# Bias tables, reciprocals and pieces of v in fewer, larger transfers, with v in DRAM by columns of the grid

## The chip, the cores and the metric

The kernel runs on one core of a Trainium2 chip. The time is the device time of one execution in microseconds (us). The engines of the core are PE (TensorE, the matmuls; PEld is its weight load), DVE (VectorE), ACT (ScalarE), POOL (GpSimd) and SP (SyncE), which does no arithmetic here and issues the transfers (DMAs) between DRAM and the on-chip buffers. The transfers run on 16 DMA engines that all queues share.

## The reference, cut to what matters

One layer with two parallel branches over 512 tokens (8 rows by 64 columns of a grid) and 1024 channels. The input is normalised, scaled and shifted to h; h goes through eight projections of 1024 columns each, and the branches meet in a gated sum, an output projection and a final norm.

```
h = rms_norm(x, g_pre) * (1 + scl) + shift
xa, za, q, k, v, zb, ga, gb = split(h @ w_in)
y_a = recurrence(conv(xa)) * silu(za) @ w_pa
y_b = neighbourhood_attention(q, k, v, rpb) * silu(zb) @ w_pb
merged = sigmoid(ga) * y_a + sigmoid(gb) * y_b
out = rms_norm(x + gate * (merged @ w_o), g_final)
```

In the attention (16 heads of 64 channels) each token looks at all 8 rows and at a window of 16 columns near its own. Scores get a bias from `rpb`, by the difference of rows and of columns; the softmax is taken over the 128 keys of the window.

## The kernel before, in words

Every matmul product is formed from a high and a low part of both operands: three passes, hi*hi, hi*lo, lo*hi. A projection by one 128-column tile of a weight (`proj`, line 689) loads 512 KB (`wraw`), casts it on ACT (`whi`), takes the difference on DVE or POOL (`wlo`), and then issues 24 matmuls of 512 columns into one bank called `acc`.

The program comes from a planner (`Plan`, line 99): each piece of work is an `op` with an engine, an estimated cost, a rank and its buffers, and the planner simulates the engines and gives each engine a fixed order. Loads have ranks that say how far ahead of their use they go, and `after`, which holds them until a given projection has begun (`gate_of`). SBUF is cut into `NS` slots of 512 columns and `NW` slots of 1024. All loads and stores but two are issued by SP, in its fixed order. Transfers use eight completion semaphores in turn (the planner keeps as many lanes, line 264), so that a transfer is issued only when the one eight places ahead of it has landed.

The order of the work:

- h is formed, and v = h @ w_v is accumulated in eight banks (`hx`), 128 tokens by 512 channels each.
- `vout` (line 666) copies each bank as high and low parts, side by side, into `va` (128 tokens by 1024 numbers) and stores it to DRAM, in `vscr0` (heads 0 to 7) or `vscr1` (heads 8 to 15). This is eight stores of 512 KB.
- For each group g of two pairs of heads there are six projections (q, k, z of each pair, lines 939 to 947), then the scores of both pairs, and the softmax and the product with v (`attend`), mixed by the planner with the projections of the next group. `bias` (line 722) loads the bias table of a pair (`braw`), from which POOL makes three tiles `nb` by subtraction from a mask.
- `load_v` (line 750) reads v back from `vscr` in the form that the product wants, with the 128 partitions holding 16 columns of the grid by 8 rows: eight tiles `vt` for each group, for four blocks of queries. Two of the tiles are half zero, by a memset on POOL.
- The reciprocals of the softmax sums are put into DRAM (`rscr`, line 894) and read back as `rcx`, each row to 64 partitions (lines 895 to 897).
- After that come the recurrent branch, mixed with the product by `w_pb`, the gates, the product by `w_pa`, and the output.

The first six projections are named here by their place: q0, k0, z0 of the first pair, q1, k1, z1 of the second. The weights of q0, k0, z0 and q1 are loaded before the eight stores of v, and those of k1 and z1 behind them in SP's order.

Of the kernel before, what the change touches and what calls it, by code (L numbers as in the profile page):

```python
# [13 lines left out]
P = 128  # L14
S = 512
# [11 lines left out]
BIG = 1e30  # L27


NS, NW = 36, 32  # L30
WARM = 60

SLACK = 3
QP, QE, BD = 1, 1, 0
LIMITS = {"hx": 8, "acc": 3, "sp": 8, "pt": 2, "pv": 2, "mi": 2, "hd": 3, "gt": 8}


# [295 lines left out]
def layer(ctx, tc, x, x_t, par, w_m, w_g, bc_gate, w_v, w_in, w_blk, rpb, amask, w_pa, w_pb, w_o, g_final, out):  # L333
# [8 lines left out]
    def op(eng, cost, fn, rank, name="", **kw):  # L342
        return pl.op(eng, cost, fn, HEAD.get(name, rank), name=name, **kw)
# [7 lines left out]
    def T(name, dt=F32):  # L351
        return pl.tile("s", lambda i: sb.tile([P, S], dt, tag=f"s{i}", name=nm(name)))

    def W(name, dt=F32):
        return pl.tile("w", lambda i: sb.tile([P, D], dt, tag=f"w{i}", name=nm(name)))
# [15 lines left out]
    def load(t, dst, src, rank, size, after=(), spare=0, r=(), late=0.0, name="load"):  # L371

        return op("SP", 0.45, lambda e: nc.sync.dma_start(dst(), src() if callable(src) else src), rank,  # L373
                  r=r, w=[t], after=after, spare=spare, size=size, late=late or SLACK * (rank > 7.9), name=name)
# [8 lines left out]
    def mm(o, a, b, first, last):  # L383
        nc.tensor.matmul(o, a, b, start=first, stop=last)  # L384
# [6 lines left out]
    def whole(t):  # L391
        return lambda: t.ap
# [268 lines left out]
    main.append(ops[4])  # L661


    vscr = [pl.fixed(dp.tile([2, S, 512], F32, name=f"vscr{n}")) for n in range(2)]

    def vout(u, rank):
        n, t = u
        a = W("va", F32R)

        def view(off, step):  # L670
            part = list(a.ap.ap)[0]
            return bass.AP(a.ap.tensor, a.ap.offset + off, [part, [256, 4], [step, 2], [1, 64]])
        src = lambda: vps[u].ap.rearrange("p (a b c) -> p a b c", a=4, b=2)
        op("ACT", act(512), lambda e: nc.scalar.copy(view(0, 192), src()), rank, r=[vps[u]], w=[a], name="voh")
        op("DVE", dve(512), lambda e: nc.vector.tensor_tensor(view(64, 64), src(), view(0, 192).bitcast(F32), op=ALU.subtract),
           rank, r=[vps[u]], rw=[a], name="vol")
        dst = vscr[n].ap[:, t * P:(t + 1) * P, :].rearrange("g p c -> p g c")
        op("SP", 0.6, lambda e: nc.sync.dma_start(dst, a.ap.bitcast(F32).rearrange("p (g c) -> p g c", g=2)), rank - 3,
           r=[a], w=[vscr[n]], size=524288, name="vout")

    for u in VU:
# [2 lines left out]
    def gate_of(n, back):  # L684
        return [main[max(0, n - back)]] if n - back >= 0 else []
# [36 lines left out]

    def bias(pr, rank, after):
        raw = T("braw")
        rv = lambda: raw.ap.rearrange("p (h f) -> p h f", h=2)
        base = RPB_L - 1 - (PAD + 2 * pr * RPB_N + RPB_C * (ROWS - 1) + 7 + 255)
        for h in range(2):
            src = bass.AP(rpb.tensor, rpb.offset + base - h * RPB_N, [[RPB_C, ROWS], [1, 16], [1, 256]])
            load(raw, lambda h=h: rv()[:, h, :], src, rank - 4, 131072, after=after, spare=4, name="bias")
        res = []  # L730
        for v0, w, m0 in ((0, 32, 0), (8, 24, 32), (0, 24, 56)):
            nb = T("nb")
            res.append(nb)
            for h in range(2):
                def f(e, h=h, nb=nb, v0=v0, w=w, m0=m0):
                    part = list(raw.ap.ap)[0]
                    mv = msk.ap[:, m0:m0 + w].unsqueeze(1).to_broadcast([P, ROWS, w])
                    view = bass.AP(raw.ap.tensor, raw.ap.offset + h * 256 + 255 - v0, [part, [-RPB_C, ROWS], [-1, w]])
                    o = nb.ap.rearrange("p (h f) -> p h f", h=2)[:, h, :ROWS * w].rearrange("p (r c) -> p r c", c=w)
                    nc.gpsimd.tensor_tensor(o, mv, view, op=ALU.subtract)  # L740
                op("POOL", pool_(ROWS * w), f, rank - 1, r=[raw, msk], w=[nb], after=after, spare=2, name="nb")
        return res
# [4 lines left out]

    PIECES = {0: ((0, 0), (16, 0)), 1: ((8, 0), (24, 0)), 2: ((24, 0), (40, 0)), 3: ((40, 64), (48, 0))}

    def load_v(g, after):  # L750
        for b in (0, 3, 1, 2):
            for j, (c0, r0) in enumerate(PIECES[b]):

                a = vt[g, b, j] = T("vt", F32R)
                n = 64 if (b, j) in ((0, 1), (3, 0)) else P
                src = vscr[g // 2].ap[g % 2].rearrange("(r c) n -> c r n", r=ROWS)[c0:c0 + n // 8]
                load(a, lambda a=a, r0=r0, n=n: a.ap[r0:r0 + n, :].bitcast(F32), src, 8 + 6 * g - 1.5 + 0.1 * (b > 0), n * 2048,
                     r=[vscr[g // 2]], after=after, spare=3, name="vt")
                if n == 64:
                    op("POOL", 0.7, lambda e, a=a, r0=r0: nc.gpsimd.memset(a.ap[64 - r0:P - r0, :].bitcast(F32), 0.0), 8 + 6 * g - 1.5,  # L760
                       w=[a], after=after, spare=3, name="vz")

    ybh, ybl = {}, {}
    rcs = [const(f"rc{i}", [P, 32]) for i in range(2)]
# [39 lines left out]
    def attend(pr, sps, z, nbt, pos, pos0):  # L804
# [3 lines left out]
        def half(bs):  # L808
# [10 lines left out]
            for members in groups:  # L819
# [12 lines left out]
                for i, (b, h) in enumerate(members):  # L832
                    def f(e_, i=i, b=b, h=h, pv2=pv2):
                        c = 2 * bs.index(b) + h
                        nc.scalar.activation(pv2(i), pv2(i), AF.Exp, bias=mn.ap[:, c:c + 1], scale=-1.0,  # L835
                                             accum_out=sm.ap[:, 2 * b + h:2 * b + h + 1])
                    op("ACT", act(nk, 1, True), f, rk - 0.25, r=[mn, pt_], w=[pt_, sm], name="exp")
                ptp, nt = B("pt"), nk // 64

# [14 lines left out]
                def f(e_, members=members, ppv=ppv):  # L854
                    for i, (b, h) in enumerate(members):
                        e = bs.index(b)
                        for j in range(2):
                            mm(pv[h].ap[:, e * 256:(e + 1) * 256], vt[pr // 2, b, j].ap[:, off + h * P:off + (h + 1) * P],
                               ppv()[:, (i if edge else 2 * i) + j].rearrange("p s q -> p (s q)"), j == 0, j == 1)
                op("PE", 0.49, f, rk - 0.4, r=[pp] + [vt[pr // 2, b, j] for b in dict(members) for j in range(2)],  # L860
                   w=[pv[h] for h in dict((h, b) for b, h in members)], name="pv")

            vp = T("vp")
# [28 lines left out]
        scr = pl.fixed(dp.tile([32, P], F32, name=f"rscr{pr}"))  # L892
        op("DVE", 0.5, recip, pos - 0.3, r=[sm], w=[rc, rct], name="rc")
        op("SP", 0.5, lambda e: nc.sync.dma_start(turned(scr.ap), rct.ap[:, :32]), pos - 3, r=[rct], w=[scr], size=16384, late=SLACK, name="rcs")
        for h in range(2):
            src = bass.AP(scr.ap.tensor, scr.ap.offset + h * P, [[0, 64], [2 * P, 4], [1, P]])
            load(rcx, lambda h=h: rcx.ap[H[h], :].rearrange("p (b q) -> p b q", b=4), src, pos - 3, 131072, r=[scr], name="rcl", late=1.0)
        op("DVE", dve(512), lambda e: nc.vector.tensor_tensor(rbc(sz.ap), rbc(sz.ap), nat(rcx.ap), op=ALU.mult),
           pos - 0.3, r=[rcx], rw=[sz], lock=True, name="szr")
        op("DVE", dve(512), lambda e: nc.vector.tensor_tensor(rbc(sz.ap), nat(yt.ap), rbc(sz.ap), op=ALU.mult), pos + 0.5, r=[yt],  # L900
# [36 lines left out]
    for g in range(4):  # L937
        sets, zs, nbs = [], [], []
        for pr in (2 * g, 2 * g + 1):
            n0 = len(main)  # L940
            nbs.append(bias(pr, n0 + BD * (1 - pr % 2), gate_of(n0, 2) if pr else [main[6]]))
            if pr % 2 == 0:
                load_v(pr // 2, gate_of(n0, 2) if pr else [])
            q = proj(w_in[16 + pr], hhl, hll, LO_A if pr else "DVE")
            k = proj(w_in[24 + pr], hhl, hll, LO_A)
            zs.append(proj(w_in[32 + pr], hhl, hll, LO_A))
            sets.append(split(q, k))
        pos = k[0] + 0.6 + QP
        for i, sps in enumerate(scores(sets, pos, ends[-1:] if QE else [])):
            attend(2 * g + i, sps, zs[i], nbs[i], pos + 3 * i, pos)  # L950
# [378 lines left out]
```

## Time and profile before

| | us |
|---|---|
| median of 3 runs (lowest, highest) | 561.11 (560.77, 564.41) |
| the profiled execution's own time | 561.85 |
| its span in the profile | 560.1 |
| PE busy in the span | 550.8 |
| DVE, ACT, POOL busy | 392.7, 322.1, 99.0 |
| transfers of SP's queue | 82.76 MB, 45.2% of the 16 engines' span |

The times in the profile start at the span's start. A row of the chain of waits or of the timeline gives the start, the duration, the engine, the line, what was written from what, and how many instructions stand behind it. A row of a view by windows gives the busy time of each engine in that window with its instructions, the granted share of the TensorE clock, the mean busy share of the 16 DMA engines, and the GB/s that they moved.

### The profile page before, as it was taken

Reading aid. Unit: us, or ns where it says so; the run is one execution under the profiler, and the core shown is the slowest. Engines: PE = TensorE matmul, PEld = TensorE weight load, DVE = VectorE, ACT = ScalarE, POOL = GpSimd, SP = SyncE. Lnnn points to the kernel's source line nnn. Section 1 sums busy time; section 2 is a strip of 40 time slices with the busy share of each in tenths; the row PEclk is TensorE's granted clock in tenths of the full one; section 3 lists DMA queues with packets and bytes.
Section 4 is the critical chain, followed back from the end, with each engine's and each line's share of the span. In section 5 each row is a group of like instructions: output and inputs, shape, how many; then the busy total and the mean of one; then the engine's idle time right before and its main releaser. Section 6 shows DMA issues by size and latency. Waiting matters only on the chain.

```text
span 560.1 us, 7705 instructions
## 1 busy us (share of the span) xinstructions
PE 550.8 (98%) x2773; PEld 458.0 (82%) x2773; DVE 392.7 (70%) x712; ACT 322.1 (58%) x560; POOL 99.0 (18%) x97
## 2 busy tenths in 40 slices
PE   8999999999999999999999999999999999999995
PEld 8888888788888888887887888888788888888885
DVE  5998723684884886897569648866967897469523
ACT  6542523862763763777965984995698243223243
POOL 1102539453553540000000000000000000000220
PEclk9999999999999999999999999999999999999998
DMA  8993899439249244034333134032319452380002
GB/s 302 409 407 109 308 272 286 128 109 235 66 120 248 59 135 149 2 97 151 112 113 95 39 112 142 28 114 75 114 59 361 144 188 75 130 321 1 0 39 113
DMA packets 36509, 83.58 MB, mean 149 GB/s; under 512 B 4607, under 2 KB 11895, under 8 KB 36471
## 3 DMA queue, kind: packets, MB, share of 16 engines
q1 hardware_dynamic: 36192, 82.76, 45.2%
q8 instruction: 22, 0.36, 0.3%
q10 hardware_dynamic: 279, 0.32, 0.2%
q14 instruction: 16, 0.13, 0.1%
HBM read 76.65 MB, written 6.42 MB: 148 GB/s over the span
## 4 chain that ended last, share of the span: by engine, by line
PE 96%; DMA 2%; DVE 0%; SPq 0%; ACT 0%; POOL 0%; issue 0%; POOLq 0%
PE acc L384 78%; PE hx L384 8%; PE pv L384 3%; PE pt L842 2%; PE gt L384 2%; PE sp L384 2%; DMA wv<-in_w_v_dram 1%; DMA xT<-in_x_t_dram 1%; SPq L373 0%; POOL vl L381 0%; PE mi L384 0%; DVE yo L1216 0%; ACT vh L378 0%; DVE pp L850 0%; ACT pp L848 0%
## 5 line engine op out<-in xcount | busy, mean ns | idle before, releaser
L384 PE MATMUL acc<-hhl,whi 128*128 128x512 f32 x784 | 244.7, 393 | 0.0
L384 PEld LDWEIGHTS acc<-hhl,whi 128*128 128x128 f32 x784 | 143.7, 188 | 27.6 <-issue 0.4
L384 PE MATMUL acc<-hhl,wlo 128*128 128x512 f32 x392 | 152.9, 390 | 0.0
L384 PEld LDWEIGHTS acc<-hhl,wlo 128*128 128x128 f32 x392 | 73.6, 188 | 15.8
L378 ACT CAST whi<-wraw 128x1024 fp32r<-128x1024 f32 x72 | 74.2, 1044 | 9.1 <-DMA wraw<-in_w_in_dram 8.5
L1195 POOL TENSOR_TENSOR yo<-yo,gfin 128x512 f32<-128x512 f32 x6 | 8.0, 1339 | 338.0 <-ACT xr L1192 337.9
L381 POOL TENSOR_TENSOR wlo<-wraw,whi 128x1024 fp32r<-128x1024 f32 x23 | 56.1, 2444 | 63.6 <-ACT whi L378 49.4
L381 DVE TENSOR_TENSOR wlo<-wraw,whi 128x1024 fp32r<-128x1024 f32 x49 | 59.4, 1220 | 8.2 <-ACT whi L378 8.0
L384 PE MATMUL acc<-woh,mhl 128*128 128x512 f32 (+1 forms) x144 | 40.4, 365 | 0.0
L384 PE MATMUL acc<-yahl,whi 128*128 128x512 f32 x128 | 39.4, 389 | 0.0
L384 PE MATMUL acc<-ybhl,whi 128*128 128x512 f32 x128 | 39.4, 389 | 0.0
L740 POOL TENSOR_TENSOR nb<-msk,braw 128x192 f32<-128x192 f32 (+1 forms) x48 | 27.7, 610 | 35.6 <-DMA braw<-in_rpb_dram 29.4
L835 ACT ACTIVATE p<-p,mn 128x192 f32<-128x192 f32 (+1 forms) x64 | 30.5, 478 | 5.9 <-DVE mn L828 5.8
L384 PE MATMUL hx<-vh,hhl 128*128 128x512 f32 x112 | 33.5, 389 | 0.0
L828 DVE CUSTOM_DVE_ANT_0 p<-sp,nb 128x192 f32<-128x192 f32 (+1 forms) x64 | 31.6, 608 | 0.9 <-PE sp L384 0.7
L1070 DVE SCALAR_TENSOR_TENSOR gm<-gm,acc 128x512 f32<-128x512 f32 x16 | 11.0, 687 | 28.6 <-PE acc L384 28.5
L384 PEld LDWEIGHTS acc<-woh,mhl 128*128 128x128 f32 x144 | 26.1, 189 | 4.4
L384 PEld LDWEIGHTS acc<-yahl,whi 128*128 128x128 f32 x128 | 24.0, 188 | 5.0
L384 PEld LDWEIGHTS acc<-ybhl,whi 128*128 128x128 f32 x128 | 24.0, 188 | 5.0
L976 DVE SCALAR_TENSOR_TENSOR xc<-acc,prm,xc 128x511 f32<-128x511 f32 (+1 forms) x24 | 18.0, 749 | 12.3 <-ACT xc L969 11.7
L850 DVE TENSOR_TENSOR pp<-pt,pp 128x384 fp32r<-128x384 f32 (+1 forms) x32 | 19.5, 625 | 10.1 <-ACT pp L848 9.8
L384 PE MATMUL acc<-wol,mhl 128*128 128x512 f32 (+1 forms) x72 | 26.3, 365 | 0.0
(202 smaller groups left out, 960.7 us busy)
## 6 DMA issues: line engine op xcount, KB each, us to landing
wraw<-in_w_in_dram SPq DMA_DIRECT2D x56, 512.0 KB, 5.6
wc<-in_w_m_dram SPq DMA_DIRECT2D x14, 512.0 KB, 9.1
vt<-vscr SPq DMA_DIRECT2D x24, 256.0 KB, 7.8
vscr<-va SPq DMA_DIRECT2D x8, 512.0 KB, 5.3
wraw<-in_w_pb_dram SPq DMA_DIRECT2D x8, 512.0 KB
wraw<-in_w_pa_dram SPq DMA_DIRECT2D x8, 512.0 KB, 7.6
wr<-in_w_g_dram SPq DMA_DIRECT2D x16, 256.0 KB, 3.9
wo<-in_w_o_dram SPq DMA_DIRECT2D x8, 512.0 KB, 3.7
```

The costliest lines, as they stand in the source:

```text
L378: return lambda e: nc.scalar.copy(o(), i()) if e == "ACT" else nc.vector.tensor_copy(o(), i())
L381: return lambda e: ENGINE[e].tensor_tensor(o(), a(), b().bitcast(F32), op=ALU.subtract)
L384: nc.tensor.matmul(o, a, b, start=first, stop=last)
L740: nc.gpsimd.tensor_tensor(o, mv, view, op=ALU.subtract)
L828: nc.vector.tensor_tensor_reduce(out=o, in0=v(spv(h, e)[:, :nk]), in1=v(nb[:, h, :nk]), scale=1.0, scalar=3e38, op0=ALU.add, op1=ALU.min, ...
L835: nc.scalar.activation(pv2(i), pv2(i), AF.Exp, bias=mn.ap[:, c:c + 1], scale=-1.0, accum_out=sm.ap[:, 2 * b + h:2 * b + h + 1])
L842: nc.tensor.transpose(ptp.ap[:, j * P:(j + 1) * P], pt_.ap[:, j * P:(j + 1) * P], ident.ap)
L850: op("DVE", dve(nt * P), lambda e_, ppv=ppv, pv4=pv4: nc.vector.tensor_tensor(ppv()[:, :, 1, :], pv4(), ppv()[:, :, 0, :].bitcast(F32), op ...
L976: nc.vector.scalar_tensor_tensor(a, b, wcol, a, op0=ALU.mult, op1=ALU.add)
L1070: op("DVE", dve(512), lambda e: nc.vector.scalar_tensor_tensor(t.ap, t.ap, 1.0, o.ap, op0=ALU.add, op1=ALU.mult), n - 1.9, r=[o], rw=[t], ...
L1195: op(("DVE", "POOL"), (dve(w), pool_(w)), lambda e: ENGINE[e].tensor_tensor(y(), y(), gfin[n].ap[:, gs], op=ALU.mult), rank + 0.1, r=[gfin ...
```

## The change

Five things are altered. The stores of v go to a `vscr` that has one row of 1024 numbers for each token, with the tokens ordered by columns of the grid (64 columns, and 8 rows within each); one store now covers two rows of the grid, written as 2 by 64 rows of 4 KB. The tiles `vt` are read from 128 consecutive rows, some of them two at a time into one buffer of 1024 columns, and one tile serves two blocks: five loads for a group instead of eight, ranked by the position of the group's second k. The bias table of a pair is laid out in full on the host and read in one load of 256 KB instead of two of 128 KB. The reciprocals are read back in one load of 256 KB, 2 by 64 rows of 2 KB, instead of two. There are two slots of 512 columns fewer and one of 1024 more.

```diff
-NS, NW = 36, 32
+NS, NW = 34, 33
...
+VP, VG = 4, 3
...
-    vscr = [pl.fixed(dp.tile([2, S, 512], F32, name=f"vscr{n}")) for n in range(2)]
+    vscr = [pl.fixed(dp.tile([S, D], F32, name=f"vscr{n}")) for n in range(2)]
...
-        dst = vscr[n].ap[:, t * P:(t + 1) * P, :].rearrange("g p c -> p g c")
-        op("SP", 0.6, lambda e: nc.sync.dma_start(dst, a.ap.bitcast(F32).rearrange("p (g c) -> p g c", g=2)), rank - 3,
+        dst = vscr[n].ap.rearrange("(c r) n -> r c n", r=ROWS)[2 * t:2 * t + 2]
+        op("SP", 0.6, lambda e: nc.sync.dma_start(dst, a.ap.bitcast(F32)), rank - 3,
            r=[a], w=[vscr[n]], size=524288, name="vout")
...
-        for h in range(2):
-            src = bass.AP(rpb.tensor, rpb.offset + base - h * RPB_N, [[RPB_C, ROWS], [1, 16], [1, 256]])
-            load(raw, lambda h=h: rv()[:, h, :], src, rank - 4, 131072, after=after, spare=4, name="bias")
+        load(raw, whole(raw), rpb[pr], rank - 4, 262144, after=after, spare=4, name="bias")
...
-                src = vscr[g // 2].ap[g % 2].rearrange("(r c) n -> c r n", r=ROWS)[c0:c0 + n // 8]
-                load(a, lambda a=a, r0=r0, n=n: a.ap[r0:r0 + n, :].bitcast(F32), src, 8 + 6 * g - 1.5 + 0.1 * (b > 0), n * 2048,
-                     r=[vscr[g // 2]], after=after, spare=3, name="vt")
...
+    def load_v(g, pos, after):
+        rows = vscr[g // 2].ap[:, g % 2 * 512:g % 2 * 512 + 512]
+        kw = dict(r=[vscr[g // 2]], after=after, spare=3, name="vt")
+        for (b0, j0), (b1, j1) in (((0, 0), (3, 1)), ((1, 0), (1, 1))):
+            a = W("vt", F32R)
+            c0, c1 = PIECES[b0][j0][0], PIECES[b1][j1][0]
+            src = rows[c0 * ROWS:c0 * ROWS + P]
+            src = bass.AP(src.tensor, src.offset, [[D, P], [D * ROWS * (c1 - c0), 2], [1, 512]])
+            load(a, lambda a=a: a.ap.rearrange("p (j n) -> p j n", j=2).bitcast(F32), src, pos + 0.1 * b1, 524288, **kw)
...
+        vt[g, 2, 0] = vt[g, 1, 1]
+        for b, j in ((0, 1), (3, 0), (2, 1)):
...
+            load(a, lambda a=a, r0=r0, n=n: a.ap[r0:r0 + n, :].bitcast(F32), rows[c0 * ROWS:c0 * ROWS + n], pos + 0.1 * (b == 2), n * 2048, **kw)
...
-        for h in range(2):
-            src = bass.AP(scr.ap.tensor, scr.ap.offset + h * P, [[0, 64], [2 * P, 4], [1, P]])
-            load(rcx, lambda h=h: rcx.ap[H[h], :].rearrange("p (b q) -> p b q", b=4), src, pos - 3, 131072, r=[scr], name="rcl", late=1.0)
+        src = bass.AP(scr.ap.tensor, scr.ap.offset, [[512, 2], [0, 64], [1, 512]])
+        load(rcx, whole(rcx), src, pos - 3, 262144, r=[scr], name="rcl", late=1.0)
...
-            if pr % 2 == 0:
-                load_v(pr // 2, gate_of(n0, 2) if pr else [])
...
+        load_v(g, k[0] - VP, [main[k[0] - VG]])
...
-        "rpb": np.concatenate([pad, f("rpb")[None, ::-1], pad], axis=1),
+        "rpb": rpb,
```

SP's order at the stores of v, before: the last two weights loaded ahead of the stores (z0, q1), the eight stores (128 by 2 by 512 numbers each), the weights of k1 and z1, and the first tile of v.

```order
L373 DMA wraw_125_575<-in_w_in_dram 128x1024
L373 DMA wraw_131_611<-in_w_in_dram 128x1024
L678 DMA vscr0_87<-va_133_620 128x2x512
L678 DMA vscr0_87<-va_135_627 128x2x512
L678 DMA vscr0_87<-va_136_633 128x2x512
L678 DMA vscr0_87<-va_137_640 128x2x512
L678 DMA vscr1_88<-va_138_647 128x2x512
L678 DMA vscr1_88<-va_139_655 128x2x512
L678 DMA vscr1_88<-va_141_664 128x2x512
L678 DMA vscr1_88<-va_143_673 128x2x512
L373 DMA wraw_148_700<-in_w_in_dram 128x1024
L373 DMA wraw_149_706<-in_w_in_dram 128x1024
```

The same place of the change.

```order
L374 DMA wraw_122_566<-in_w_in_dram 128x1024
L374 DMA wraw_129_606<-in_w_in_dram 128x1024
L680 DMA vscr0_87<-va_131_615 2x64x1024
L680 DMA vscr0_87<-va_133_622 2x64x1024
L680 DMA vscr0_87<-va_134_628 2x64x1024
L680 DMA vscr0_87<-va_135_635 2x64x1024
L680 DMA vscr1_88<-va_136_642 2x64x1024
L680 DMA vscr1_88<-va_137_650 2x64x1024
L680 DMA vscr1_88<-va_139_659 2x64x1024
L680 DMA vscr1_88<-va_141_668 2x64x1024
L374 DMA wraw_146_695<-in_w_in_dram 128x1024
L374 DMA wraw_147_701<-in_w_in_dram 128x1024
```

The stores stand at the same place; what differs is the shape that each writes, 2 by 64 rows of 1024 numbers in place of 128 by 2 rows of 512.

SP's order a little later, before: the weights of the next group's first three projections, the bias of the third pair, the eight tiles of v of the second group, and more weights; the rows begin at the third of those weights.

```order
L373 DMA wraw_168_830<-in_w_in_dram 128x1024
L373 DMA braw_175_868<-in_rpb_dram 128x1x256 x2
L373 DMA vt_178_878<-vscr0_87 128x1x512
L373 DMA vt_174_866<-vscr0_87 64x1x512
L373 DMA vt_181_889<-vscr0_87 64x1x512
L373 DMA vt_183_896<-vscr0_87 128x1x512
L373 DMA vt_184_898<-vscr0_87 128x1x512
L373 DMA vt_186_906<-vscr0_87 128x1x512
L373 DMA vt_188_913<-vscr0_87 128x1x512
L373 DMA vt_189_915<-vscr0_87 128x1x512
L373 DMA wraw_190_921<-in_w_in_dram 128x1024
L373 DMA wraw_194_935<-in_w_in_dram 128x1024
```

The same place of the change, from the same weight on.

```order
L374 DMA wraw_165_822<-in_w_in_dram 128x1024
L374 DMA braw_172_862<-in_rpb_dram 128x512
L374 DMA wraw_175_868<-in_w_in_dram 128x1024
L374 DMA wraw_183_908<-in_w_in_dram 128x1024
L374 DMA wraw_206_1020<-in_w_in_dram 128x1024
L374 DMA braw_226_1103<-in_rpb_dram 128x512
L374 DMA vt_225_1101<-vscr0_87 64x512
L374 DMA vt_229_1114<-vscr0_87 64x512
L374 DMA vt_231_1123<-vscr0_87 128x2x512
L374 DMA vt_232_1126<-vscr0_87 128x512
L374 DMA vt_233_1133<-vscr0_87 128x2x512
```

Three weights and the bias of the fourth pair have moved ahead of the second group's tiles of v.

POOL's order around the low parts (`wlo`) of the weights of z0, q1, k1 and z1, before, with the memsets of the second group's tiles of v and the bias tiles `nb` of the second pair.

```order
L381 TENSOR_TENSOR wlo_147_695<-wraw_125_575,whi_145_682 128x1024
L381 TENSOR_TENSOR wlo_150_722<-wraw_131_611,whi_146_692 128x1024
L381 TENSOR_TENSOR wlo_169_832<-wraw_148_700,whi_166_821 128x1024
L381 TENSOR_TENSOR wlo_172_851<-wraw_149_706,whi_171_839 128x1024
L760 MEMSET vt_174_866 64x512
L740 TENSOR_TENSOR nb_177_876<-msk_74,braw_163_808 128x256 x2
L740 TENSOR_TENSOR nb_182_894<-msk_74,braw_163_808 128x192 x2
L740 TENSOR_TENSOR nb_187_911<-msk_74,braw_163_808 128x192 x2
```

The same place of the change.

```order
L382 TENSOR_TENSOR wlo_145_690<-wraw_122_566,whi_143_677 128x1024
L382 TENSOR_TENSOR wlo_148_717<-wraw_129_606,whi_144_687 128x1024
L768 MEMSET vt_152_736 64x512
L768 MEMSET vt_153_743 64x512
L382 TENSOR_TENSOR wlo_166_824<-wraw_146_695,whi_163_813 128x1024
L738 TENSOR_TENSOR nb_169_843<-msk_74,braw_150_730 128x256 x2
L738 TENSOR_TENSOR nb_170_852<-msk_74,braw_150_730 128x192 x2
L738 TENSOR_TENSOR nb_173_864<-msk_74,braw_150_730 128x192 x2
L382 TENSOR_TENSOR wlo_178_878<-wraw_147_701,whi_168_831 128x1024
```

The six `nb` of the second pair have moved ahead of the `wlo` of z1, and two memsets stand ahead of that of k1. The compute engines have the same instructions as before in number and shape; SP issues 206 in place of 234.

More of the change, by code (lines that the diff above doesn't have):

```diff
@@ L724, in bias @@
         raw = T("braw")
-        rv = lambda: raw.ap.rearrange("p (h f) -> p h f", h=2)
-        base = RPB_L - 1 - (PAD + 2 * pr * RPB_N + RPB_C * (ROWS - 1) + 7 + 255)
-        for h in range(2):
-            src = bass.AP(rpb.tensor, rpb.offset + base - h * RPB_N, [[RPB_C, ROWS], [1, 16], [1, 256]])
-            load(raw, lambda h=h: rv()[:, h, :], src, rank - 4, 131072, after=after, spare=4, name="bias")
+        load(raw, whole(raw), rpb[pr], rank - 4, 262144, after=after, spare=4, name="bias")
         res = []
@@ L748, in layer @@
     PIECES = {0: ((0, 0), (16, 0)), 1: ((8, 0), (24, 0)), 2: ((24, 0), (40, 0)), 3: ((40, 64), (48, 0))}
[L750 to L755, printed above, removed]
-                src = vscr[g // 2].ap[g % 2].rearrange("(r c) n -> c r n", r=ROWS)[c0:c0 + n // 8]
-                load(a, lambda a=a, r0=r0, n=n: a.ap[r0:r0 + n, :].bitcast(F32), src, 8 + 6 * g - 1.5 + 0.1 * (b > 0), n * 2048,
-                     r=[vscr[g // 2]], after=after, spare=3, name="vt")
-                if n == 64:
-                    op("POOL", 0.7, lambda e, a=a, r0=r0: nc.gpsimd.memset(a.ap[64 - r0:P - r0, :].bitcast(F32), 0.0), 8 + 6 * g - 1.5,
-                       w=[a], after=after, spare=3, name="vz")
+    def load_v(g, pos, after):
[7 more added lines that the diff above has]
+            load(a, lambda a=a: a.ap.rearrange("p (j n) -> p j n", j=2).bitcast(F32), src, pos + 0.1 * b1, 524288, **kw)
+            for m, bj in enumerate(((b0, j0), (b1, j1))):
+                vt[g, *bj] = a, (lambda a=a, m=m: a.ap[:, m * 512:(m + 1) * 512])
+        vt[g, 2, 0] = vt[g, 1, 1]
+        for b, j in ((0, 1), (3, 0), (2, 1)):
+            c0, r0 = PIECES[b][j]
+            a = T("vt", F32R)
+            vt[g, b, j] = a, whole(a)
+            n = 64 if b != 2 else P
+            load(a, lambda a=a, r0=r0, n=n: a.ap[r0:r0 + n, :].bitcast(F32), rows[c0 * ROWS:c0 * ROWS + n], pos + 0.1 * (b == 2), n * 2048, **kw)
+            if n == 64:
+                op("POOL", 0.7, lambda e, a=a, r0=r0: nc.gpsimd.memset(a.ap[64 - r0:P - r0, :].bitcast(F32), 0.0), pos,
+                   w=[a], after=after, spare=3, name="vz")
     ybh, ybl = {}, {}
@@ L835, in f @@
                         nc.scalar.activation(pv2(i), pv2(i), AF.Exp, bias=mn.ap[:, c:c + 1], scale=-1.0,
-                                             accum_out=sm.ap[:, 2 * b + h:2 * b + h + 1])
+                                             accum_out=sm.ap[:, 4 * h + b:4 * h + b + 1])
                     op("ACT", act(nk, 1, True), f, rk - 0.25, r=[mn, pt_], w=[pt_, sm], name="exp")
@@ L857, in f @@
                         for j in range(2):
-                            mm(pv[h].ap[:, e * 256:(e + 1) * 256], vt[pr // 2, b, j].ap[:, off + h * P:off + (h + 1) * P],
+                            mm(pv[h].ap[:, e * 256:(e + 1) * 256], vt[pr // 2, b, j][1]()[:, off + h * P:off + (h + 1) * P],
                                ppv()[:, (i if edge else 2 * i) + j].rearrange("p s q -> p (s q)"), j == 0, j == 1)
-                op("PE", 0.49, f, rk - 0.4, r=[pp] + [vt[pr // 2, b, j] for b in dict(members) for j in range(2)],
+                op("PE", 0.49, f, rk - 0.4, r=[pp] + [vt[pr // 2, b, j][0] for b in dict(members) for j in range(2)],
                    w=[pv[h] for h in dict((h, b) for b, h in members)], name="pv")
@@ L1298 @@
     ]).reshape(120, P)
-    pad = np.zeros((1, PAD), np.float32)
+    at = (lambda r, q, h, w: RPB_L - 1 - (PAD + RPB_C * (ROWS - 1) + 7 + 255) - h * RPB_N + RPB_C * r + q + w)(
+        *np.ogrid[:ROWS, :16, :2, :256]).reshape(P, 2, 256)
+    rpb = np.pad(f("rpb")[::-1], PAD)
+    rpb = np.stack([rpb[at - 2 * i * RPB_N] for i in range(NH // 2)]).reshape(NH // 2, P, 512)
     arrays = {
```

## The prediction

> **What bounds the kernel now.** I read the page's busy times first, then what PE waited for, then the chain that ended last. The page, then PE's waits (total us, times, longest):
>
> ```profile
> span 560.1 us, 7705 instructions
> PE 550.8 (98%) x2773; PEld 458.0 (82%) x2773; DVE 392.7 (70%) x712; ACT 322.1 (58%) x560; POOL 99.0 (18%) x97
> ...
> PE hx L502 <- POOL epsc L450: 1.5, 1, 1.5
> PE pv L384 <- DVE pp L850: 1.1, 1, 1.1
> PE hx L384 <- POOL vl L381: 0.2, 1, 0.2
> ```
>
> PE is the bound: it waits 2.8 us in all, 1.7 of them in the first 17 us, which the change doesn't touch. Only the wait of 1.1 us lies in the attention. No transfer that is made cheaper can give more than that, while any new hole on PE is paid in full. So the question is what could make PE wait. The chain, PE's timeline (first matmuls of q0, k0 and k1) and SP's timeline show where PE's cover is thin:
>
> ```profile
> 60.42 32.64 PE acc L384 x144
> ...
> 60.25 0.39 PE L384 MATMUL acc<-hh,whi 128*128 128x512 f32 x1
> 65.69 0.39 PE L384 MATMUL acc<-hh,whi 128*128 128x512 f32 x1
> 82.01 0.39 PE L384 MATMUL acc<-hh,whi 128*128 128x512 f32 x1
> ...
> 34.07 1.61 SPq L373 DMA_DIRECT2D wraw<-in_w_in_dram  x2
> 39.19 1.68 SPq L373 DMA_DIRECT2D wraw<-in_w_in_dram  x2
> 57.03 8.47 SPq L678 DMA_DIRECT2D vscr<-va  x8
> 65.55 2.56 SPq L373 DMA_DIRECT2D wraw<-in_w_in_dram  x2
> 68.20 8.16 SPq L373 DMA_DIRECT2D vt<-vscr  x8
> 82.99 8.85 SPq L373 DMA_DIRECT2D vt<-vscr  x8
> 91.98 2.24 SPq L373 DMA_DIRECT2D wraw<-in_w_in_dram  x3
> ```
>
> A projection takes PE 65.69 - 60.25 = 5.44 us. Four weights are loaded before the eight stores of v; they feed PE until 60.25 + 4 x 5.44 = 82.01. The fifth, that of k1, is issued behind all eight stores and needed at 82.01.
>
> **The stores of v.** How many DMA engines does a transfer use? The view by windows answers: the second number from the end is the mean busy share of the 16 engines, the last the GB/s.
>
> ```profile
> 57.00:58.00 1.00, 1.00 (x7) 0.80 (x6) 0.95 (x3) 0.87 (x3) 1.00 (x3) 1.00 0.05 20
> 58.00:60.00 2.00, 2.00 (x10) 1.68 (x9) 2.00 (x4) 1.68 (x4) 1.60 (x4) 1.00 1.02 376
> ...
> 166.60:167.10 0.50, 0.50 (x4) 0.40 (x3) 0.50 (x1) 0.00 (x0) 0.50 (x1) 1.00 0.48 119
> 240.90:241.20 0.30, 0.30 (x3) 0.26 (x2) 0.30 (x2) 0.00 (x0) 0.00 (x0) 1.00 0.32 50
> 543.00:544.10 1.10, 1.10 (x6) 0.91 (x5) 0.31 (x2) 0.86 (x3) 0.09 (x1) 1.00 0.99 410
> 553.20:554.20 1.00, 0.44 (x4) 0.23 (x2) 0.49 (x2) 0.00 (x0) 0.00 (x0) 1.00 1.03 422
> ...
> 164.53 1.33 SPq L373 DMA_DIRECT2D braw<-in_rpb_dram  x2
> 239.66 0.56 SPq L894 DMA_DIRECT2D rscr<-rct  x1
> 542.04 10.51 SPq L1223 DMA_DIRECT2D out_dram<-yo  x3
> ```
>
> From 58 to 60 the old stores of v move (128 by 2 by 512), with a share of 1.02: all 16 engines. In the window at 166.6 a bias load moves, whose source is counted 8 by 16 by 256 (line 728): 0.48, eight engines of 16. In that at 240.9 the store of the reciprocals moves, 4 by 32 by 32 (lines 712 and 894): 0.32, nearer to four engines than to eight, with short rows that overlap in the record. The share falls with the outermost count of the side that has fewer, 128, 8, 4, though the side in SBUF has 128 partitions in the last two as well. The new stores write 2 by 64 by 1024. I read that as two engines.
>
> The Trainium skill has this as a rule (DMA: Bandwidth & Descriptors, section on why a DMA increments its semaphore by 16): the number of engines is the largest up to 16 that divides the outermost counts of both sides, here 2. The same page's rules for kernel authors speak for the change, since they want many small transfers made into one large one; the rows above say which of the two rules decides for this store.
>
> The price of an engine: the stores of the output at 543 have rows of 4 KB, as the new stores of v have, and 410 / 16 = 25.6 GB/s an engine. A store of 524,288 bytes on two engines is 262,144 / 25.6 = 10.2 us, and eight of them, one behind the other on the same two engines, 81.9 us. At the 422 GB/s of 553.2 it would be 79.5, at the 376 of the old stores 89.2; I take 81.9, for the row length. The first store is issued at 57.03 and moves from about 57.9 (a share of 0.05 in the window from 57 to 58), so the eighth ends at 139.8.
>
> What is late then: the weight of k1 is spread over all 16 engines, and its part on those two stands behind the stores: 8 rows of 4 KB, 32,768 / 25.6 = 1.3 us, so it lands at 141.1. That an engine takes SP's transfers in the order of their issue is assumed here; no row shows it by itself, and the case without it is a rival below. Then come its cast and its low part, for which ACT's and POOL's timelines have the times:
>
> ```profile
> 72.03 1.05 ACT L378 CAST whi<-wraw 128x1024 fp32r<-128x1024 f32 x1
> 73.16 2.39 POOL L381 TENSOR_TENSOR wlo<-wraw,whi 128x1024 fp32r<-128x1024 f32 x1 [6.33 <-ACT whi L378]
> ```
>
> From 72.03 to 73.16 + 2.39 = 75.55 is 3.5 us, so PE can begin k1 at 144.6 where it began at 82.01: a hole of 62.6 us. Behind the waiting cast on ACT are queued the tanh of z0 and the cast of z1, behind POOL's `wlo` the six `nb` of the second pair, behind PE's matmul everything. All of that waits with it and nothing else is made late: the other weights and the tiles of v land within a few us after 141, ahead of their use. On POOL, `nb` now stands ahead of the `wlo` of z1: 6 x 610 ns (the group of `nb`, below) + 2.39 = 6.1 us against the 5.44 of k1 on PE; the next paragraph's slow start covers the 0.6.
>
> After a hole PE starts slowly, as at the start of the program:
>
> ```profile
> 1.51 3.35 PE L502 MATMUL hx<-onesc 128*128 128x128 f32 x14 [1.51 <-POOL epsc L450]
> 4.93 2.64 PE L435 MATMUL hx<-par_sb,ident 120*128 120x128 f32 x16
> 7.41 2.62 PE L502 MATMUL hx<-onesc 128*128 128x128 f32 x22
> ...
> L740 POOL TENSOR_TENSOR nb<-msk,braw 128x192 f32<-128x192 f32 (+1 forms) x48 | 27.7, 610 | 35.6 <-DMA braw<-in_rpb_dram 29.4
> ```
>
> 14 matmuls take 0.239 us each, then 16 take 0.165, then 22 take 0.119: against the last pace 14 x 0.12 + 16 x 0.046 = 2.4 us are lost. I charge 2.4 (0 to 5 as bounds).
>
> **The other edits.** The wait of 1.1 us goes back to a cast of a weight that came late behind the second group's reads of v:
>
> ```profile
> 99.76 1.05 ACT L378 CAST whi<-wraw 128x1024 fp32r<-128x1024 f32 x1 [3.83 <-DMA wraw<-in_w_in_dram]
> ```
>
> Those reads now stand behind three more weights, so I give -1.1 (0 at the other end). The 28 transfers fewer save issue time of some 0.6 us each on SP, which waits for PE and ACT for most of the span: 0. The bias as 128 rows of 2 KB and the reads of v from consecutive rows get all engines; PE never waited for either: 0. The reciprocals, read as 2 by 64 by 512, get two engines: 131,072 / 25.6 = 5.1 us, where two loads landed in 3.7 each:
>
> ```profile
> DMA to landing us min/median/max: 3.1/3.7/4.7
> 260.73 0.68 DVE L898 TENSOR_TENSOR sz<-sz,rcx 128x512 f32<-128x512 f32 x1
> 262.83 0.69 DVE L381 TENSOR_TENSOR ybhl<-sz,ybhl 128x512 fp32r<-128x512 f32 x1
> 270.55 0.61 PE L384 MATMUL acc<-ybhl,whi 128*128 128x512 f32 x2
> ```
>
> The last pair's product is ready at 263.5 and PE takes it up at 270.55 at the earliest, which hides some 2 us: 0, and up to 2 if that cover is gone. Weights queued behind such a read come up to 5.1 later, with a projection or more in hand: 0. The slots change the planner's order after the attention, but not the work: 0.
>
> **The sum.** 62.6 + 2.4 - 1.1 = 63.9. The profiled execution took 561.85 (span 560.1 and 1.75 around it), so 625.8; it stands 0.74 above the median of 561.11, so 625.0 for the median.
>
> **The rivals.**
>
> *The stores still run on all engines.* The number could follow the 128 partitions of the side in SBUF. For it speaks that the amount and the row count divide well; against it the 0.48 and 0.32 above, where the SBUF side had 128 partitions. Then the eighth store ends near 69, the weight of k1 is there in time, and only the 1.1 us is left: 560.0, not slower. It decides from about nine engines up: with n engines the store's work is 163.8 / n, and 57.9 + 163.8 / n + 1.3 + 3.5 stays under 82.0 when n is 8.5 or more.
>
> *Weights pass the stores on those two engines.* Then k1 isn't late. But SP issues a transfer only when the one eight places ahead has landed, so the two weights, the bias and the five tiles of v behind the stores go out one for each store that ends, the last at 139.8, and the seventh weight behind it. That lands some 2.5 us later (issue, 0.9 as for the first store, and 1.3 of moving, both above), and 3.5 more make 145.8. PE needs it after the scores:
>
> ```profile
> 93.06 2.98 PE sp L384 x48
> ```
>
> That is at 96.0, a hole of 49.8: 49.8 + 2.4 - 1.1 = 51.1, and 612.2. For it speaks that no row shows the order on an engine; against it, that the stores' rate of 376 GB/s is still there (381) after the two weights are issued at 65.55:
>
> ```profile
> 66.00:68.00 2.00, 2.00 (x11) 1.65 (x10) 1.81 (x6) 0.48 (x1) 0.83 (x1) 1.00 1.03 381
> ```
>
> Rows of 4 KB move at 410 or more, so these are still the stores, whose 4.19 MB at 380 last until 69. The Trainium skill says the same (DMA: Bandwidth & Descriptors, section on queues, rings and completion order): an engine takes up the work of one queue in its order.
>
> *The two engines are slower than that.* The reads of v have rows 128 KB apart, and the engines were busy but slow:
>
> ```profile
> 74.00:76.00 2.00, 2.00 (x11) 1.65 (x10) 0.00 (x0) 0.00 (x0) 1.55 (x1) 1.00 1.10 196
> ```
>
> 196 / 16 = 12.3 GB/s an engine would make the eight stores 171 us, 89 more: 714. The new rows are 32 KB apart on each engine, but the stores in the trace, at 376 to 422, show no such loss; this case is mostly a tail to the forecast.
>
> **How the numbers follow.** Forecast 0.80; all engines 0.12; weights pass 0.04; slower engines 0.04. The forecast's own range is 81.9 less 2.4 or plus 7.3, the clock 0 to 5, the 1.1 and the 2: about 620 to 638. The range reaches down over the case of 612.2 and up into the slow case, 607 to 650, and leaves out the case of 560.0 and the end of the tail, some 0.15. A measurement here tells about 1% (the runs before spread by 0.65%). Slower by more: 0.88; within: 0.11; faster: 0.01, since 1.1 us is 0.2%.
>
> **What would show it.** From 58 to about 140 us the share of the DMA engines near 0.13 at about 51 GB/s, apart from short bursts of weights; PE without a matmul from 82 to about 145, released by POOL's `wlo`, and behind that a cast on ACT that waited for a weight; PE's busy time unchanged but for 2 or 3 us. A share near 1 from 58 to 68 would make the whole forecast wrong; a hole that begins at 96 in place of 82 would mean that weights pass.

## The result and the profile after

The changed kernel took **626.59 us** (median of 6 runs, 626.33 to 626.96) beside 562.35 us of the kernel before in the same comparison (6 runs, 560.77 to 564.41): a ratio of **1.1139, interval 1.1111 to 1.1167**. It is slower by 64 us; the forecast was 625.0 in a range of 607 to 650. The profiled execution took 626.87 us, 2.3 of it around the span.

The page of the changed kernel: busy times, then in 40 slices the granted clock of PE, the share of the DMA engines, and the GB/s. All line numbers are 1 to 8 higher than those of before.

```profile
span 624.6 us, 7671 instructions
...
PE 553.7 (89%) x2773; PEld 459.5 (74%) x2773; DVE 389.3 (62%) x712; ACT 322.4 (52%) x560; POOL 101.8 (16%) x97
...
PEclk9999975556999999999999999999999999999999
DMA  8990111158334442451243223322232836183002
GB/s 321 408 371 9 54 52 53 52 185 292 128 106 142 149 152 84 160 171 41 81 135 114 97 84 101 100 87 69 100 102 71 306 106 225 34 287 117 1 34 102
```

PE's instructions are the same 2773, its busy time rises by 2.9 us (550.8 to 553.7), and the span by 64.5. A slice is 15.6 us: in slices 5 to 8, from 62 to 125 us, the DMA engines move 52 to 54 GB/s at a share of one tenth. PE's waits in the changed kernel, in the form of those of before:

```profile
PE acc L385 <- ACT whi L379: 60.5, 1, 60.5
PE hx L503 <- POOL epsc L451: 1.5, 1, 1.5
PE acc L385 <- POOL wlo L382: 1.3, 1, 1.3
PE hd L495 <- DVE sq L489: 0.6, 1, 0.6
```

One hole of 60.5 + 1.3 = 61.8 us is new, the wait of 1.1 us for `pv` is gone. PE's timeline at the hole, the last matmul of q1 and the first of k1:

```profile
81.63 0.39 PE L385 MATMUL acc<-hhl,wlo 128*128 128x512 f32 x1
142.54 0.79 PE L385 MATMUL acc<-hh,whi 128*128 128x512 f32 x1 [60.53 <-ACT whi L379]
143.13 0.63 PE L385 MATMUL acc<-hl,whi 128*128 128x512 f32 x1
145.04 0.80 PE L385 MATMUL acc<-hh,wlo 128*128 128x512 f32 x1 [1.28 <-POOL wlo L382]
```

What released it stands on the timelines of ACT, first, and of POOL. The number in brackets is the idle time before the instruction, and what ended it:

```profile
141.44 1.04 ACT L379 CAST whi<-wraw 128x1024 fp32r<-128x1024 f32 x1 [69.67 <-DMA wraw<-in_w_in_dram]
```

```profile
142.62 2.36 POOL L382 TENSOR_TENSOR wlo<-wraw,whi 128x1024 fp32r<-128x1024 f32 x1 [74.75 <-ACT whi L379]
144.94 3.40 POOL L738 TENSOR_TENSOR nb<-msk,braw 128x256 f32<-128x256 f32 x6
148.30 7.09 POOL L382 TENSOR_TENSOR wlo<-wraw,whi 128x1024 fp32r<-128x1024 f32 x3
```

And SP's timeline of the changed kernel (start, duration in the queue, what it issued, how many), and behind it the chain of waits over the same stretch:

```profile
56.87 53.63 SPq L680 DMA_DIRECT2D vscr<-va  x8
110.55 17.78 SPq L374 DMA_DIRECT2D wraw<-in_w_in_dram  x2
```

```profile
77.18 9.70 SPq L680
86.98 9.70 SPq L680
96.77 9.69 SPq L680
106.56 3.94 SPq L680
110.55 30.87 DMA wraw<-in_w_in_dram
142.62 2.37 POOL wlo L382
```

The eight stores, which SP issued in 8.47 us before, now hold it for 53.63: one stands in its issue for 9.70 us. SP begins to issue the weight of k1 at 110.55 and stands 16.69 us in that one issue as well; the weight lands 30.87 us after 110.55, at 141.4. The windows of the changed kernel (the last three numbers are PE's clock, the share of the DMA engines and the GB/s), and last, for comparison, the window of k1 in the kernel before:

```profile
72.00:80.00 8.00, 8.00 (x37) 6.64 (x36) 1.04 (x5) 0.00 (x0) 0.00 (x0) 1.00 0.13 52
90.00:100.00 10.00, 0.00 (x0) 0.00 (x0) 0.00 (x0) 0.00 (x0) 0.00 (x0) 0.50 0.13 52
130.00:138.00 8.00, 0.00 (x0) 0.00 (x0) 0.00 (x0) 0.00 (x0) 0.00 (x0) 0.50 0.76 244
142.54:153.01 10.47, 9.19 (x24) 6.80 (x25) 1.38 (x2) 5.01 (x6) 10.39 (x10) 0.59 1.01 368
150.00:154.00 4.00, 4.00 (x17) 3.22 (x16) 0.16 (x1) 2.61 (x3) 4.00 (x3) 0.86 0.94 354
...
82.01:87.45 5.44, 5.44 (x25) 4.50 (x24) 0.69 (x1) 1.64 (x2) 3.29 (x6) 1.00 0.98 325
```

0.13 x 16 is two engines, at 52 GB/s 26 each. By the slices this holds until about 125 us; from 130 to 138 the share is 0.76, while SP issues what stands behind the stores. In the next two rows PE has restarted: k1's matmuls, from 142.54 to the first of z1 at 153.01, keep it busy for 9.19 us in place of 5.44, at a clock of 0.50 for most of the time. The mean of 0.86 over 150 to 154 puts the change to 1.00 near 151.1.

### The profile page after: what moved, and what is told of

Its sections match the earlier page's. It is cut to its first block, busy times and chain, and to the rows that moved or that the text cites. A ratio compares the mean times of both kernels' runs of the same rounds, so it can differ in the third digit from the quotient of the medians.

```text
span 624.6 us, 7671 instructions
## 1 busy us (share of the span) xinstructions
PE 553.7 (89%) x2773; PEld 459.5 (74%) x2773; DVE 389.3 (62%) x712; ACT 322.4 (52%) x560; POOL 101.8 (16%) x97
## 4 chain that ended last, share of the span: by engine, by line
PE 84%; SPq 6%; DMA 5%; DVE 2%; ACT 1%; POOL 0%; issue 0%; POOLq 0%; DVEq 0%; ACTq 0%
PE acc L385 67%; PE hx L385 7%; SPq L680 6%; DMA wraw<-in_w_in_dram 5%; PE pv L385 2%; PE gt L385 2%; PE pt L850 2%; PE sp L385 2%; DMA par_sb<-in_par_dram 1%; ACT whi L379 0%; POOL wlo L382 0%; DVE lt L923 0%; PE hx L503 0%; PE hd L495 0%; PE hd L550 0%
## 5 line engine op out<-in xcount | busy, mean ns | idle before, releaser
L385 PE MATMUL acc<-hh,whi 128*128 128x512 f32 x56 | 23.1, 413 | 60.5 <-ACT whi L379 60.5
L890 DVE SCALAR_TENSOR_TENSOR sz<-sz,acc 128x512 f32<-128x512 f32 x8 | 5.5, 686 | 87.6 <-ACT sz L889 87.6
L385 PEld LDWEIGHTS acc<-hh,whi 128*128 128x128 f32 x56 | 10.6, 189 | 64.8 <-ACT whi L379 60.9
L738 POOL TENSOR_TENSOR nb<-msk,braw 128x192 f32<-128x192 f32 (+1 forms) x48 | 29.6, 652 | 31.4 <-DMA braw<-in_rpb_dram 31.4
```

## The experiments

The theory: the number of engines of a store follows the outermost count of its shape, the two engines make the eight stores last until 140, and the weight of k1 stands behind them in SP's queue. The rivals asked about were the layout of v or its new reads as the cause; a cost that doesn't depend on the cover ahead of the stores; and, for the order of the queue, an engine that takes the transfers of all queues as they come.

**1. The stores on all engines.** Each store is cut into the two rows of the grid that it covers, 64 by 1024 each; all else is the changed kernel.

```diff
-        dst = vscr[n].ap.rearrange("(c r) n -> r c n", r=ROWS)[2 * t:2 * t + 2]
-        op("SP", 0.6, lambda e: nc.sync.dma_start(dst, a.ap.bitcast(F32)), rank - 3,
+        def put(e):
+            for j in range(2):
+                dst = vscr[n].ap.rearrange("(c r) n -> r c n", r=ROWS)[2 * t + j]
+                nc.sync.dma_start(dst, a.ap[64 * j:64 * j + 64].bitcast(F32))
+        op("SP", 0.6, put, rank - 3,
```

> The changed kernel with each store of v cut into two of 64 rows (one row of the grid each), so that the outermost count is 64 and not 2; layout in DRAM, bytes, reads of v and everything else as changed. Engines theory (the number of engines follows the outermost count): share of the 16 engines near 1 from 58 to 69, no hole on PE at 82, time 560 to 562. Spacing theory (rows of 4 KB written 32 KB apart are slow by themselves, as the old reads were at 196 GB/s): 4.19 MB at 196 GB/s is 21.4 us, the hole at 82 is about 2 us, 564. If another part of the change made the hole (the reads of v, the slots, the planner's order): still about 626.

Measured: 560.66 us (560.27 to 561.99, 12 runs) beside 561.92 of the kernel before, ratio 0.998 (0.9971 to 0.999). PE's waits are down to one, that at the start of the program, so the hole of 2 us of the spacing theory is not there either; that view, then windows, then SP's timeline of this kernel:

```profile
PE hx L503 <- POOL epsc L451: 1.5, 1, 1.5
```

```profile
58.00:60.00 2.00, 2.00 (x11) 1.65 (x10) 1.96 (x4) 1.78 (x4) 2.00 (x5) 1.00 0.74 154
60.00:64.00 4.00, 4.00 (x19) 3.31 (x18) 2.30 (x6) 3.74 (x6) 1.69 (x2) 1.00 0.86 278
```

```profile
57.38 14.89 SPq L682 DMA_DIRECT2D vscr<-va  x16
72.33 1.58 SPq L374 DMA_DIRECT2D wraw<-in_w_in_dram  x2
```

The same bytes to the same rows, cut at the outermost count of 2: the whole loss is gone. The sixteen halves are issued in 14.89 us (0.93 each), so they run below the 376 GB/s of the old stores (the share is 0.74 and 0.86, where near 1 was expected), and the weight of k1 is issued at 72.33 in place of 65.55, which its need at 82 still covers.

**2. The reciprocals too.** As 1, and the read of the reciprocals cut in two, each of 64 partitions.

```diff
-        src = bass.AP(scr.ap.tensor, scr.ap.offset, [[512, 2], [0, 64], [1, 512]])
-        load(rcx, whole(rcx), src, pos - 3, 262144, r=[scr], name="rcl", late=1.0)
+        def get(e):
+            for h in range(2):
+                src = bass.AP(scr.ap.tensor, scr.ap.offset + 512 * h, [[0, 64], [1, 512]])
+                nc.sync.dma_start(rcx.ap[H[h], :], src)
+        op("SP", 0.45, get, pos - 3, r=[scr], w=[rcx], size=262144, late=1.0, name="rcl")
```

> As the run with the stores on all engines, and the read of the reciprocals cut in two as well, each to 64 partitions, so that it has all engines. My theory: the two-engine read of the reciprocals is hidden, so the same time as the run with the stores alone within 0.3 us, 560 to 562; the reads land in about 3.5 us and not 6. Rival (the slow read delays weights queued behind it): 1 to 2 us faster than the run with the stores alone.

Measured: 560.67 us (560.17 to 561.15, 12 runs), ratio 0.9971 (0.9955 to 0.9987): the same as 1. What the cut changes is seen on DVE alone. In kernel 1, as in the changed kernel, the products wait for `rcx`; the row of kernel 1, in the view of that tile (us, times), has no counterpart in kernel 2:

```profile
  DMA rcx<-rscr: 7.1, 4
```

So the read on two engines is late for DVE by 7.1 us in four places, and none of it reaches PE. Kernels 1 and 2 are the two that come out below the kernel before, by 0.2 to 0.3%, which is the size of the wait that went (1.1 of 561 us) but less than the 1% taken here as telling.

**3 and 4. Three engines and one.** The halves of 1 are cut once more, into 57 and 7 rows (the largest divisors up to 16 are 3 and 7), and into 61 and 3 rows (1 and 3). The edit of kernel 3 against 1; in kernel 4 the bounds are (0, 61) and (61, 64):

```diff
-                nc.sync.dma_start(dst, a.ap[64 * j:64 * j + 64].bitcast(F32))
+                for c0, c1 in ((0, 57), (57, 64)):
+                    nc.sync.dma_start(dst[c0:c1], a.ap[64 * j + c0:64 * j + c1].bitcast(F32))
```

> The changed kernel with each row of the grid stored in pieces of 57 and 7 rows. By the largest divisor up to 16, 57 gives 3 engines and 7 gives 7, so the busiest engine moves 19 + 1 = 20 rows of 4 KB for each of 16 halves: 20 x 16 x 0.159 = 50.9 us, from 57.9 to 108.8; with 1.3 for the weight and 3.5 for cast and low part PE starts k1 at 113.6 where 82 was: a hole near 32, time 561 + 31.6 + 2.9 - 1.1 = 594. If counts that do not divide are spread over all engines anyway: 561.

> The changed kernel with each row of the grid stored in pieces of 61 and 3 rows. 61 is prime: one engine, 61 + 1 rows for each of 16 halves, 62 x 16 x 0.159 = 157.7 us, from 57.9 to 215.6; PE starts k1 at 220.4, a hole of 138, time 561 + 138.4 + 2.9 - 1.1 = 701. If counts that do not divide are spread over all engines anyway: 561.

Measured: **595.0 and 700.27 us**, one run each. A window while the stores move, and from PE's timeline the first matmul with `wlo` behind the hole, both of kernel 3 and then both of kernel 4:

```profile
72.00:80.00 8.00, 8.00 (x37) 6.60 (x36) 0.80 (x3) 0.00 (x0) 0.00 (x0) 1.00 0.23 84
```

```profile
114.77 0.79 PE L385 MATMUL acc<-hh,wlo 128*128 128x512 f32 x1 [1.28 <-POOL wlo L382]
```

```profile
72.00:80.00 8.00, 8.00 (x37) 6.64 (x36) 1.28 (x6) 0.04 (x1) 0.00 (x0) 1.00 0.07 28
```

```profile
218.92 0.80 PE L385 MATMUL acc<-hh,wlo 128*128 128x512 f32 x1 [1.28 <-POOL wlo L382]
```

Counting the rows of 4 KB that the busiest engine gets over all stores (taking that the small pieces use it too):

| kernel | pieces of a store | rows on the busiest engine | PE resumes at (us) | time (us) |
|---|---|---|---|---|
| 1 | 64, 64 | 64 | no hole | 560.66 |
| 3 | 57, 7, 57, 7 | 8 x 2 x (19 + 1) = 320 | 114.77 | 595.0 |
| changed | 2 x 64 | 8 x 64 = 512 | 145.04 | 626.59 |
| 4 | 61, 3, 61, 3 | 8 x 2 x (61 + 1) = 992 | 218.92 | 700.27 |

From 320 to 512 rows PE resumes 30.27 us later, 0.158 us a row; from 512 to 992 rows 73.88 later, 0.154 a row. That is 26.0 and 26.6 GB/s for one engine, where the prediction took 25.6 from the stores of the output. The windows agree: of the 64 rows of a half, 20 and 62 go to the busiest engine, so it moves 84 x 20 / 64 = 26.3 and 28 x 62 / 64 = 27.1 GB/s. Everything else in these kernels is alike, so the busiest engine's share sets the time.

**5. Two engines in the kernel before.** Layout, reads, bias and reciprocals of before; only the stores are cut by partitions into pieces that get 2, 2 and 4 engines.

```diff
-        op("SP", 0.6, lambda e: nc.sync.dma_start(dst, a.ap.bitcast(F32).rearrange("p (g c) -> p g c", g=2)), rank - 3,
+        def put(e):
+            for p0, p1 in ((0, 62), (62, 124), (124, 128)):
+                nc.sync.dma_start(dst[p0:p1], a.ap[p0:p1].bitcast(F32).rearrange("p (g c) -> p g c", g=2))
+        op("SP", 0.6, put, rank - 3,
```

> The kernel before, with one edit: each store of v is cut by partitions into 62, 62 and 4 rows of the tile, outermost counts whose largest divisors up to 16 are 2, 2 and 4. Layout of v in DRAM, the reads of v, the bias and the reciprocals stay those of the kernel before. Theory (two engines are the whole cause, the new layout has no part in it): 62 partitions by 2 rows of 2 KB are 62 packets an engine, two such pieces and the small one make about 126 packets of 2 KB an engine and store, at the 85 ns that a packet of 2 KB took in the kernel before 10.7 us a store and 86 for eight; the last ends near 143.6, PE starts k1 near 148, a hole of 66, and the time is 628 to 632. Rival (the layout by columns of the grid or the new reads of v cause the loss): 561 to 563.

Measured: 633.45 us (one run). PE's waits in this kernel, and a window:

```profile
PE acc L384 <- ACT whi L378: 62.0, 1, 62.0
PE pv L384 <- DVE pp L853: 4.6, 1, 4.6
...
PE acc L384 <- POOL wlo L381: 1.2, 1, 1.2
```

```profile
90.00:100.00 10.00, 0.00 (x0) 0.00 (x0) 0.00 (x0) 0.00 (x0) 0.00 (x0) 0.50 0.13 52
```

The same share, the same rate and, at 63.2 us, the same hole in a kernel that has none of the new layout: the layout and the reads have no part in the loss. The time is 1.45 us above the expected range, and the size was missed at two points: the hole is 3 us shorter than expected (52 GB/s where packets of 2 KB at 85 ns had given 48), and the wait for `pv` is 4.6 us in place of 1.1, since here the second group's reads of v stand ahead of three weights, as in the kernel before.

**6. Six weights ahead.** The changed kernel, with the weights of k1 and z1 loaded ahead of the stores.

```diff
-        load(raw, whole(raw), w, n - 5, 524288, after=gate_of(n, 5), spare=1,
+        early = n in (13, 14)
+        load(raw, whole(raw), w, 0 if early else n - 5, 524288, after=[main[6]] if early else gate_of(n, 5), spare=1,
```

> The changed kernel, with the weights of k1 and z1 loaded ahead of the eight stores of v, so that six weights in place of four cover PE. Theory (the loss is what is left of the stores' time when PE's loaded weights run out): no hole at 82; PE goes on through k1, z1 and the scores to about 96 and then waits for the seventh weight, which is issued behind the stores and lands at 140 to 146; with the 3.5 us of its cast and low part the hole is 48 to 53, and the time 609 to 616. Rival (a fixed cost of the new stores, whatever is loaded ahead of them): 625 to 627, with the hole of the changed kernel.

Measured: 620.52 us (one run). PE's and ACT's timelines of this kernel at the hole:

```profile
94.30 0.28 PE L385 MATMUL sp<-kh,ql 64*128 64x256 f32 x2
150.34 0.53 PE L385 MATMUL sp<-kh,qh 64*128 64x192 f32 x2 [55.76 <-ACT kh L783]
...
145.92 1.04 ACT L379 CAST whi<-wraw 128x1024 fp32r<-128x1024 f32 x1 [68.61 <-DMA wraw<-in_w_in_dram]
147.31 1.04 ACT L379 CAST whi<-wraw 128x1024 fp32r<-128x1024 f32 x1 [0.35 <-DMA wraw<-in_w_in_dram]
...
149.69 0.60 ACT L783 ACTIVATE kh<-acc 128x512 fp32r<-128x512 f32 x1
```

There is no hole at 82 any more, PE works through k1, z1 and half of the scores, and then stands: the loss moves with the cover, as the theory has it, and the rival with a fixed cost falls. The time, though, is 4.5 us above the expected range. Two things were missed. PE stops at 94.6 and not at 96, because the second half of the scores needs `kh`, ACT's copy of k1's result, and that stands behind the cast that waits for the seventh weight; and the copy comes 3.8 us after that weight, behind two more casts and another copy. The weight itself lands at 145.9, since the bias and five tiles of v stand ahead of it in the same queue.

**7. Two weights by another queue.** The changed kernel, with the weights of k1 and z1 issued by ACT; the stores stay on two engines and on SP's queue.

```diff
+        if n in (13, 14):
+            op("ACT", 0.45, lambda e: nc.scalar.dma_start(raw.ap, w), n - 5, w=[raw], after=gate_of(n, 5), spare=1, late=5.0, name=f"w{n}")
+        else:
...
```

> The changed kernel, with the two weights of k1 and z1 issued by ACT's queue in place of SP's; all else, the stores on two engines too, stays. If the order of SP's queue alone holds these weights (SP is blocked in issuing the stores until 110.5, and an engine takes the transfers of one queue in their order but shares itself between queues): the weights land within 10 us of their issue, PE has no hole at 82, and waits from about 96 for the seventh weight, still on SP behind the stores, that lands at 140 to 146: 609 to 616. If an engine takes the transfers of all queues in the order in which they were issued, k1's weight ends only behind the stores that were issued before it: a hole from 82, shorter or as long as that of the changed kernel, and 618 to 627.

Measured: 622.52 us (one run). ACT's timeline of this kernel (its queue is named ACTq), then PE's waits:

```profile
60.73 0.36 ACTq L697 DMA_DIRECT2D wraw<-in_w_in_dram  x1
61.84 0.33 ACTq L697 DMA_DIRECT2D wraw<-in_w_in_dram  x1
...
67.96 1.05 ACT L379 CAST whi<-wraw 128x1024 fp32r<-128x1024 f32 x1 [1.59 <-DMA wraw<-in_w_in_dram]
70.58 1.05 ACT L379 CAST whi<-wraw 128x1024 fp32r<-128x1024 f32 x1 [1.57 <-DMA wraw<-in_w_in_dram]
```

```profile
PE sp L385 <- ACT kh L785: 58.3, 1, 58.3
```

Issued at 60.73 and 61.84, both weights are there by 67.96 and 70.58, about 7 and 9 us later, through the same 16 engines, two of which had the backlog of stores. The same weight in SP's queue took 30.87 us; 16.69 of them SP stood in its issue, and from the end of that it still took 14.2. So a queue's transfers keep their order on an engine, and those of another queue pass. The Trainium skill states the same (DMA: Bandwidth & Descriptors, section on queues, rings and completion order): each issuing queue has its own ring on every engine, a ring is consumed in order, and an engine takes turns between the rings that hold work for it. The trace agrees, with 7 and 9 us beside 30.87. The hole is again the one behind the scores, waiting for the seventh weight in SP's queue; the time misses its range by 6.5 us for the reasons given under 6.

## Why the prediction was right

*Two engines for the new stores.* Confirmed by the share of 0.13, and beyond the count of 2 by kernels 3 and 4 (0.23 and 0.07, and the row counts of the table), which follow the largest divisor up to 16 of the outermost count. The rival with all engines fell; it is what kernel 1 does.

*The price, 25.6 GB/s an engine and 81.9 us for eight.* 26 in the window, 26.0 and 26.6 by the slopes of the table. The weight of k1 was forecast to land at 141.1; its cast began at 141.44.

*The order of the queue.* The prediction assumed it and showed no row; kernel 7 beside the changed kernel shows it. The hole of 62.6 was 61.8: PE was released by ACT's cast first, not by POOL's `wlo` as forecast; it started k1's first two matmuls with `whi` alone and then waited 1.28 more for `wlo`, until 145.04 (forecast 144.6).

*The slow start.* 2.4 us forecast, 3.75 measured: k1 keeps PE busy for 9.19 us in place of 5.44. The rise of PE's busy time as a whole, 2.9, is smaller only because PE is busy for 0.5 us less in the first 20 us and 0.4 less behind k1. That PE would start slowly was right; the size was too small. At the program's start the slow pace lasted some 5 us (an estimate from the prediction's rows: 0.239 us a matmul from 1.51 on, 0.119 from 7.41 on, and 0.165 on average in the 16 in between); behind the hole PE worked for some 7.3 us at a clock of 0.50, and about half of such a stretch is lost. The forecast's bounds of 0 to 5 hold it.

*The wait of 1.1 us for `pv`* is gone, as forecast. Only kernel 5, which keeps the old order of the reads, has a wait there, of 4.6 us.

*The other edits at nothing.* Kernel 1 keeps them all and stands at 0.998; the reciprocals on two engines cost DVE 7 us and PE none (kernel 2). The `nb` ahead of z1's `wlo` on POOL, 3.40 us, was covered by PE's slow k1, as forecast: no wait of PE stands there.

The sum: 61.8 + 3.75 - 1.1 = 64.45, which is the span's 64.5. Up to the end of q1 nothing is lost (PE is done with it at 82.02, and k1 began at 82.01 before); z1 starts 65.56 us later (153.01 less 87.45), and of that 1.1 is won back behind it. 63.9 had been forecast: the hole was 0.8 shorter and the slow start 1.35 longer, so that it came this near is in part luck.

*What was off.* The account of SP in the rival "weights pass" held that SP issues until the transfer eight places back has landed. It doesn't get that far: SP stands in the issue of a store for up to 9.70 us, and the weight of k1 was not issued by about 70, when the first store would have landed, but from 110.55 to 127.24. The number didn't suffer, because the two engines' own backlog ended later still. And that rival's 612.2 was priced too low: kernel 7, the nearest to it, took 622.52, since ACT's waiting cast also holds the copy that PE's scores need. The prediction also read the rules for kernel authors of the Trainium skill (DMA: Bandwidth & Descriptors) as speaking for the change, by their row on many small transfers. The stores of v are no such case: they are eight of 512 KB before and after, and only the rows that they write are new.

## What to carry to other kernels

Before giving a transfer a new shape, or making many into one, look at the outermost count of the shape on both sides: eight stores of 2 by 64 rows ran on two engines and cost 64 us, and the same bytes as sixteen stores of 64 rows cost nothing. The price of a transfer is the bytes of its busiest engine, here 0.154 to 0.158 us for each row of 4 KB, and it is paid by whatever stands behind it in the same queue and has the least cover, not by who reads the data. When a wait is moved rather than removed, look at what else is queued behind the waiting instruction on its engine: in kernels 6 and 7 ACT's cast also held a copy that PE's scores needed, so the hole opened in the middle of the scores and closed behind two more casts.

## What the runs showed of the hardware

A queue with a backlog on two engines blocks its issuer: SP stood for 9.7 us in each of the three stores that the chain above shows, and then for 16.69 in the weight of k1, which is spread over all engines (8 rows for each):

```profile
L374 SPq DMA_DIRECT2D wraw<-in_w_in_dram x56: 327/367/16689, 33.6 to 513.8; - x56
```

(in the changed kernel, all issues of such weights: shortest, median and longest in ns). When the last store had been issued, at 110.55, about 2.9 stores were outstanding by the rate ((140 - 110.55) / 10.2, an estimate from the rows above). How much a queue holds was not measured.

After the hole PE's slow pace lasted longer than at the program's start: its matmuls run without a gap from 145.04, and the clock goes from 0.50 to 1.00 near 151.1, 6.1 us later. The Trainium skill (TensorE: Matmul & The Clock Gate, Part 1) puts the change after at least one busy window of about 3.4 us, in windows that run freely; two such windows would hold the 6.1, one would not.
